# A hand-written order for the opening of a decoder layer, and a raised priority for one chain in its down stage

## The chip, the core and the metric

The kernel runs on one core of a Trainium2 chip. The time is that of the device for one execution, in microseconds (us). An execution under the profiler gives the trace; its own time is listed beside the runs without it.

## What is computed

One decoder layer on 512 tokens of width 1024, in float32: a half-step SwiGLU feed-forward, a mixer (block-sparse attention beside a state-space model), and a second half-step feed-forward, each between two RMS norms.

```python
def swiglu(x, w_gate, w_up, w_down):
    return (jax.nn.silu(x @ w_gate) * (x @ w_up)) @ w_down

f = swiglu(rmsnorm(h, ffn1_pre_g[l]), ffn1_w_gate[l], ffn1_w_up[l], ffn1_w_down[l])
h = h + 0.5 * rmsnorm(f, ffn1_post_g[l])
```

The hidden width is 2816, that is 22 blocks of 128. The state-space model needs tables that depend on its parameters alone: among them the powers 1 to 128 of a complex number for each of 2048 states. They are computed in the first feed-forward, between its own instructions.

## The kernel before

Every product is split in two parts for precision. A float32 operand becomes a high part (ScalarE, a copy to a narrower format) and a low part (VectorE, the operand minus its high part), and a product is three matmuls: high by high, high by low, low by high. A weight of 128 by 1024 comes by DMA into one of three raw buffers (`load`, L76) and is split by `weight` (L82): L89 on ScalarE, L90 on VectorE. A raw buffer is free for the next load when its low part has been made.

**The opening** (L1139 to L1182) handles the first two hidden blocks, that is four weights (gate and up of block 0, gate and up of block 1), called units here. The tokens lie in four blocks of 128. `turn_x` (L135) transposes the rows of one token block, in two halves of 512 columns: four transposes on TensorE, a product by the column gain on VectorE (L143), the high part on ScalarE (L145); `low_x` makes the low part. The first two token blocks are not normalised before the products: their rows are turned as they come, and their norm factor is applied later. The last two are normalised first: `norm_x` (L153) squares the rows and adds them up (`square`, on ScalarE, or on VectorE for block 3), makes the factor with a power on GpSimd (L60), scales the rows on ScalarE (L163), and gives a function that turns them.

`halves` (L214) multiplies the units in two halves of 256 tokens: first tokens 0 to 255 for all four units, then tokens 256 to 511. Its hooks turn token block 2 after the first half of unit 1, and block 3 after that of unit 2. The first half of unit 0 goes by parts, all eight high by high products, then high by low, then low by high; the others take the three products of each of the eight slices in turn. Between the halves stands `late_norm` (L179): a diagonal of the norm factors is spread over all partitions by a product with ones (L188), copied out by ScalarE (L190), then the four PSUM banks are multiplied by it (L192), then the columns of the first two token blocks (L196), whose parts are made anew (L197, L198) for the hidden blocks that follow. A unit's two halves lie in the two halves of one bank.

**The order** of TensorE and GpSimd is that of the program. VectorE, ScalarE and the DMA queue of SP are ordered by a planner, which simulates the program with costs of its own and gives each engine the ready instruction that stands first; `high_priority(PRIO)` counts an instruction as standing 400 places earlier. Within `manual_schedule` (L1156) the instructions of VectorE and ScalarE keep the program's order among themselves.

**The down stage** (L484 to L500) takes the 22 hidden blocks one by one: `split` makes the parts of a hidden block (L475 on ScalarE, L476 on VectorE), `weight` those of its down weight, and TensorE issues 24 matmuls of 512 columns into eight banks. After each block the loop draws steps from a generator, here `rest` (L710): three after the first block, two after the second, then one each. It first makes the powers by doubling, in eight steps of six VectorE instructions each (`cmul`, L557; the result is named e, its scratch ett), stores them to DRAM (L731), then makes four tables (st) from loads (f, b). From the twelfth block on, the parts of hidden blocks lie in memory that the powers held (`open_third`, L267).

Of the kernel before, what the change touches and what calls it, by code (L numbers as in the profile page):

```python
# [25 lines left out]
class Core:  # L26
    def __init__(self, tc, ctx):
# [7 lines left out]
        self.ident = self.const.tile([P, P], F32, name="ident")  # L35
# [93 lines left out]
    def open_x(self, ctx, gcol):  # L129
# [3 lines left out]
        self.gcol = gcol  # L133

    def turn_x(self, t, q, rows):  # L135
# [9 lines left out]
        nc.scalar.activation(self.xh[:, k, t * P:(t + 1) * P], f, AF.Copy)  # L145
# [6 lines left out]

    def norm_x(self, t, on_dve=False):  # L153

        nc = self.nc
        ss = self.small("ss", 2)
        xn = [self.t512("xn") for _ in range(2)]
        with self.tc.high_priority(PRIO):
            for q in range(2):
                self.square(t, q, xn[q], ss, on_dve)  # L160
            rs = self.rsqrt(ss, D * EPS)
            for q in range(2):
                nc.scalar.activation(xn[q], self.h[t][:, 512 * q:512 * q + 512], AF.Copy, scale=rs)  # L163

        def transposes():
            with self.tc.high_priority(PRIO):
                for q in range(2):
                    self.turn_x(t, q, xn[q])
                    self.low_x(t, q)
        return transposes  # L170
# [8 lines left out]
    def late_norm(self, banks):  # L179
# [4 lines left out]
        diag = self.t512("diag")  # L184
        for t in range(2):
            v.tensor_scalar(diag[:, t * P:(t + 1) * P], self.ident, self.rs[t], None, op0=OP.mult)
# [4 lines left out]
        for b in banks:  # L191
            v.tensor_tensor(b[:, :H], b[:, :H], rsb, OP.mult)  # L192
        for q in range(2):
# [4 lines left out]
            v.tensor_tensor(self.xl[:, k, :H], f, self.xh[:, k, :H].bitcast(F32), OP.subtract)  # L198

# [14 lines left out]
    def halves(self, units, hooks, by_part=False):  # L214


        for half in range(2):
            for i, (u, pb) in enumerate(units):
                if half == 0 and i == 0 and by_part:
                    pairs = ((u[0], self.xh), (u[0], self.xl), (u[1], self.xh))  # L220
                    for n, (a, b) in enumerate(pairs):
                        for k in range(NK):
                            self.nc.tensor.matmul(pb[:, :H], a[:, k * P:(k + 1) * P], b[:, k, :H],
                                                  start=n == 0 and k == 0, stop=n == 2 and k == NK - 1)
                else:
                    self.proj_T(u, pb, (half * H, half * H + H))
# [3 lines left out]
            if half == 0 and by_part:  # L230
                self.late_norm([pb for u, pb in units])
# [200 lines left out]
    def ffn(self, wgu, wd, gains, tail, hooks, first, direct, store=None):  # L432
# [19 lines left out]
        us = [(u, self.bank("gu")) for u in first]  # L452
# [34 lines left out]
        for i, k in enumerate(order):  # L487
# [11 lines left out]
            for _ in range({0: 3, 1: 2}.get(i, 1)):  # L499
                next(self.filler or iter(()), None)  # L500
# [66 lines left out]
class Tables:  # L567
# [142 lines left out]
    def rest(self, pool, wide, vec):  # L710
# [9 lines left out]
        while n < P:  # L720
            for lo in range(0, n, 32):
                m = min(32, n - lo)
                s1, s2 = (t[:, :16 * m].rearrange("p (c x) -> p c x", c=16) for t in tt)
                cmul(vec, et[0][:, :, n + lo:n + lo + m], et[1][:, :, n + lo:n + lo + m],
                     et[0][:, :, lo:lo + m], et[1][:, :, lo:lo + m],
                     et[0][:, :, n - 1:n].to_broadcast([P, 16, m]), et[1][:, :, n - 1:n].to_broadcast([P, 16, m]), s1, s2)
# [373 lines left out]
def _lay(i):  # L1100
    a = {k: np.asarray(v)[0] for k, v in i.items()}
    win, wo = a["w_in"], a["w_out"]
    out = dict(x=a["x"], ident=np.eye(P, dtype=np.float32))
# [5 lines left out]
    out["g0col"] = a["ffn1_pre_g"].reshape(NK, P).T  # L1109
# [23 lines left out]
def layer(tc, ctx, a, out):  # L1133
# [6 lines left out]
    nc.sync.dma_start(c.ident, a["ident"])  # L1140
    gcol = c.const.tile([P, NK], F32, name="gcol")
# [14 lines left out]
    with tc.manual_schedule(engines={mybir.EngineType.DVE, mybir.EngineType.Activation}):  # L1156
# [10 lines left out]
        for q in range(2):  # L1167
            for t in range(2):
                c.low_x(t, q)
# [47 lines left out]
```

## Time and profile before

| | |
|---|---|
| median of 3 runs | 936.06 us (934.13 to 937.15) |
| the profiled execution | 932.66 us, span 930.7 us |
| TensorE busy | 910.2 us, 98% of the span |
| VectorE busy | 688.8 us, 74% |
| ScalarE busy | 426.5 us, 46% |
| GpSimd busy | 58.8 us, 6% |
| mean granted TensorE clock | 0.992 |

The span runs from the first instruction of the program to the last. Engines are named as in the profile: PE is TensorE's matmuls (transposes too), PEld its weight loads, DVE VectorE, ACT ScalarE, POOL GpSimd, SP the queue that issues the DMAs. L12 is line 12 of the kernel; the line can be that of a helper. In a row of a timeline, x4 says that four like instructions were merged, and the brackets give the idle time of the engine ahead of the first of them and who ended it. The durations of neighbours overlap by a little, so the distance of their starts is shorter than a duration. A granted clock of 1.00 is 2.4 GHz, one of 0.50 is 1.2 GHz.

### The profile page before, as it was taken

Reading aid. Unit: us, or ns where it says so; the run is one execution under the profiler, and the core shown is the slowest. Engines: PE = TensorE matmul, PEld = TensorE weight load, DVE = VectorE, ACT = ScalarE, POOL = GpSimd, SP = SyncE. Lnnn points to the kernel's source line nnn. Section 1 sums busy time; section 2 is a strip of 40 time slices with the busy share of each in tenths; the row PEclk is TensorE's granted clock in tenths of the full one; section 3 lists DMA queues with packets and bytes.
Section 4 is the critical chain, followed back from the end, with each engine's and each line's share of the span. In section 5 each row is a group of like instructions: output and inputs, shape, how many; then the busy total and the mean of one; then the engine's idle time right before and its main releaser. Section 6 shows DMA issues by size and latency. Waiting matters only on the chain.

```text
span 930.7 us, 14874 instructions
## 1 busy us (share of the span) xinstructions
PE 910.2 (98%) x5815; PEld 816.6 (88%) x5815; DVE 688.8 (74%) x1179; ACT 426.5 (46%) x717; POOL 58.8 (6%) x47
## 2 busy tenths in 40 slices
PE   7899999999999899998999999999999999999997
PEld 6888899999988788987888778989999999988885
DVE  6998678888588655579999869698878887533623
ACT  5622345455422444333478756445445555423511
POOL 0600000000000001022120113000000000000000
PEclk9999999999999999999999999999999999999999
DMA  7444532332666651584433132322433333332402
GB/s 262 122 135 130 186 101 91 108 98 69 192 178 216 224 187 35 171 249 147 147 98 97 32 105 71 121 82 91 117 111 100 106 102 104 116 110 90 136 1 90
DMA packets 51718, 114.59 MB, mean 123 GB/s; under 512 B 10048, under 2 KB 21056, under 8 KB 51648
## 3 DMA queue, kind: packets, MB, share of 16 engines
q1 hardware_dynamic: 51648, 113.65, 38.9%
q8 instruction: 45, 0.74, 0.3%
q14 instruction: 25, 0.20, 0.1%
HBM read 102.62 MB, written 11.01 MB: 122 GB/s over the span
## 4 chain that ended last, share of the span: by engine, by line
PE 79%; DVE 11%; DMA 3%; ACT 3%; issue 2%; POOL 1%; SPq 1%; DVEq 0%; POOLq 0%; ACTq 0%
PE c L408 28%; PE d L204 6%; PE d L202 6%; PE d L203 6%; PE p L408 5%; DMA b<-in_bturn 2%; PE pg L202 2%; PE pu L204 2%; PE pg L204 2%; PE pu L203 2%; PE pg L203 2%; PE pu L202 2%; DVE w L90 1%; PE gu L204 1%; PE gu L202 1%
## 5 line engine op out<-in xcount | busy, mean ns | idle before, releaser
L408 PE MATMUL c<-xh,w 128*128 128x256 f32 x1024 | 180.7, 277 | 0.2 <-DVE w L287 0.2
L408 PEld LDWEIGHTS c<-xh,w 128*128 128x128 f32 x1024 | 157.0, 188 | 0.5 <-DVE w L287 0.4
L90 DVE TENSOR_TENSOR w<-w,w 128x1024 fp32r<-128x1024 f32 x93 | 114.8, 1241 | 44.6 <-ACT w L89 44.3
L89 ACT ACTIVATE w<-w 128x1024 fp32r<-128x1024 f32 x93 | 97.3, 1054 | 101.6 <-PE d L204 20.0
L408 PE MATMUL c<-xl,w 128*128 128x256 f32 x512 | 141.7, 277 | 0.0
L204 PE MATMUL d<-w,sl 128*128 128x512 f32 x352 | 137.6, 391 | 2.5 <-DVE sl L476 2.5
L202 PE MATMUL d<-w,sh 128*128 128x512 f32 x352 | 137.8, 392 | 0.0
L203 PE MATMUL d<-w,sh 128*128 128x512 f32 x352 | 137.7, 391 | 0.0
L287 DVE TENSOR_TENSOR w<-w,w 128x1024 fp32r<-128x1024 f32 x96 | 116.7, 1221 | 27.5 <-ACT w L286 27.1
L286 ACT ACTIVATE w<-w 128x1024 fp32r<-128x1024 f32 x96 | 100.2, 1058 | 67.6 <-PE c L408 40.8
L408 PE MATMUL c<-t,w 128*128 128x256 f32 x768 | 97.4, 283 | 0.1
L408 PEld LDWEIGHTS c<-xl,w 128*128 128x128 f32 x512 | 96.2, 188 | 0.0
L408 PEld LDWEIGHTS c<-t,w 128*128 128x128 f32 x768 | 94.1, 191 | 0.3 <-DVE w L287 0.3
L204 PEld LDWEIGHTS d<-w,sl 128*128 128x128 f32 x352 | 66.5, 189 | 16.8 <-DVE sl L476 2.9
L202 PEld LDWEIGHTS d<-w,sh 128*128 128x128 f32 x352 | 66.4, 189 | 13.8
L203 PEld LDWEIGHTS d<-w,sh 128*128 128x128 f32 x352 | 66.5, 189 | 13.6
L60 POOL TENSOR_TENSOR rs<-v,mhalf 128x1 f32<-128x1 f32 x24 | 19.1, 799 | 715.2 <-DVE v L56 715.2
L408 PE MATMUL p<-t,s1h 128*128 128x256 f32 x256 | 46.5, 282 | 0.0
L475 ACT ACTIVATE sh<-late 128x512 fp32r<-128x512 f32 x22 | 13.5, 630 | 60.9 <-PE d L203 60.9
L468 ACT ACTIVATE sg<-c 128x256 f32<-128x256 f32 x64 | 24.5, 382 | 34.1 <-DVE c L426 27.6
L408 PEld LDWEIGHTS p<-t,s1h 128*128 128x128 f32 x256 | 39.6, 190 | 0.0
L408 PE MATMUL p<-t,s1l 128*128 128x256 f32 x128 | 36.1, 282 | 0.0
(318 smaller groups left out, 1778.7 us busy)
## 6 DMA issues: line engine op xcount, KB each, us to landing
w<-in_wgu SPq DMA_DIRECT2D x88, 512.0 KB, 3.5
w<-in_wd SPq DMA_DIRECT2D x44, 512.0 KB, 3.7
e<-e SPq DMA_DIRECT2D x16, 256.0 KB, 3.5
w<-in_wq SPq DMA_DIRECT2D x8, 512.0 KB, 3.7
g<-in_gains SPq DMA_DIRECT2D x5, 512.0 KB, 6.0
h<-in_x SPq DMA_DIRECT2D x4, 512.0 KB, 6.0
ca<-cx SPq DMA_DIRECT2D x8, 256.0 KB, 4.4
f<-win SPq DMA_DIRECT2D x32, 64.0 KB, 3.7
```

What stands on the lines that cost most here:

```text
L60: self.nc.gpsimd.tensor_tensor(rs, v, self.mhalf, OP.pow)
L89: nc.scalar.activation(hi, raw, AF.Copy)
L90: (eng or nc.vector).tensor_tensor(lo, raw, hi.bitcast(F32), OP.subtract)
L202: nc.tensor.matmul(out, ah, bh, start=first, stop=False)
L203: nc.tensor.matmul(out, ah, bl, start=False, stop=False)
L204: nc.tensor.matmul(out, al, bh, start=False, stop=last)
L286: nc.scalar.activation(hi, src, AF.Copy)
L287: nc.vector.tensor_tensor(lo, src, hi.bitcast(F32), OP.subtract)
L408: nc.tensor.matmul(out, l[:, s], r[:, kb + k, t], start=first and k == 0 and n == 0, stop=last and k == 3 and n == 2, skip_group_check=True)
L468: nc.scalar.activation(sg, pg, AF.Silu)
L475: nc.scalar.activation(hi, hidden[k], AF.Copy)
```

## The change

The opening is written out in one order for VectorE and ScalarE; the squares of token block 0 stand before its first high parts, those of block 1 near the end, the squares of blocks 2 and 3 between the parts of weights 1 and 2. `turn_x` no longer makes the high part; `high_x` does, as a step of its own. The first halves of all four units are issued there, each by parts (`first_half`), and token blocks 2 and 3 are turned inside those of units 2 and 3, after their high by high products. `halves` then does only the second halves, and `late_norm` comes after that of unit 0, with raised priority; in it the four banks are multiplied after the columns and no longer before. The column gains come with the identity in one DMA. In the down stage the steps of the powers get raised priority, and four steps are drawn after the first block.

```diff
+    def high_x(self, t, q):
+        k = slice(4 * q, 4 * q + 4)
+        f = self.xf[t // 2][:, k, t % 2 * P:t % 2 * P + P]
+        self.nc.scalar.activation(self.xh[:, k, t * P:(t + 1) * P], f, AF.Copy)
...
         rsb = self.t512("rsb")[:, :H]
         nc.scalar.activation(rsb, pb, AF.Copy)
-        for b in banks:
-            v.tensor_tensor(b[:, :H], b[:, :H], rsb, OP.mult)
         for q in range(2):
             k = slice(4 * q, 4 * q + 4)
             f = self.xf[0][:, k]
             v.tensor_tensor(f, f, rsb.unsqueeze(1).to_broadcast([P, 4, H]), OP.mult)
             nc.scalar.activation(self.xh[:, k, :H], f, AF.Copy)
             v.tensor_tensor(self.xl[:, k, :H], f, self.xh[:, k, :H].bitcast(F32), OP.subtract)
+        for b in banks:
+            v.tensor_tensor(b[:, :H], b[:, :H], rsb, OP.mult)
...
+    def first_half(self, unit, pb, between=None):
+
+        hi, lo = unit
+        for n, (a, b) in enumerate(((hi, self.xh), (hi, self.xl), (lo, self.xh))):
+            for k in range(NK):
+                self.nc.tensor.matmul(pb[:, :H], a[:, k * P:(k + 1) * P], b[:, k, :H],
+                                      start=n == 0 and k == 0, stop=n == 2 and k == NK - 1)
+            if n == 0 and between is not None:
+                between()
+
+    def halves(self, units, hooks, begun=False):
...
+        for half in range(begun, 2):
             for i, (u, pb) in enumerate(units):
...
+                self.proj_T(u, pb, (half * H, half * H + H))
...
+                if begun and i == 0:
+                    with self.tc.high_priority(PRIO):
+                        self.late_norm([pb for u, pb in units])
...
-            for _ in range({0: 3, 1: 2}.get(i, 1)):
+            for _ in range({0: 4, 1: 2}.get(i, 1)):
                 next(self.filler or iter(()), None)
...
+                with core.tc.high_priority(PRIO):
+                    cmul(vec, et[0][:, :, n + lo:n + lo + m], et[1][:, :, n + lo:n + lo + m],
...
-    nc.sync.dma_start(c.ident, a["ident"])
-    gcol = c.const.tile([P, NK], F32, name="gcol")
-    nc.sync.dma_start(gcol, a["g0col"])
+    nc.sync.dma_start(c.identg, a["ident"])
...
+        c.turn_x(0, 0, rows(0, 0))
+        c.turn_x(0, 1, rows(0, 1))
         for q in range(2):
+            c.square(0, q, junk, ss[0], False)
+        c.high_x(0, 0)
+        c.high_x(0, 1)
+        warm_up(WARM[1])
+        c.turn_x(1, 0, rows(1, 0))
+        c.turn_x(1, 1, rows(1, 1))
+        warm_up(WARM[2])
+        c.high_x(1, 0)
+        high(0, col(0))
+        c.high_x(1, 1)
+        high(0, col(1))
         for q in range(2):
             for t in range(2):
                 c.low_x(t, q)
+        banks = [c.bank("gu") for j in range(4)]
+        low(0, col(0))
+        low(0, col(1))
+        c.first_half(w[0], banks[0])
+        high(1)
         for q in range(2):
+            c.square(2, q, xn[2][q], ss[2], False)
+        for q in range(2):
+            c.square(3, q, xn[3][q], ss[3], True)
+        rs2 = c.rsqrt(ss[2], D * EPS)
+        low(1)
+        rs3 = c.rsqrt(ss[3], D * EPS)
+        c.first_half(w[1], banks[1])
+        high(2)
+        scaled(2, rs2)
+        low(2)
+        c.first_half(w[2], banks[2], turn(2))
+        high(3)
+        low(3)
+        for q in range(2):
+            c.high_x(2, q)
+        for q in range(2):
+            c.low_x(2, q)
+        scaled(3, rs3)
+        for q in range(2):
+            c.square(1, q, junk, ss[1], False)
+        c.first_half(w[3], banks[3], turn(3))
+        for q in range(2):
+            c.high_x(3, q)
+        rs = [c.rsqrt(ss[t], D * EPS) for t in range(2)]
+        for q in range(2):
+            c.low_x(3, q)
+        c.diag = c.t512("diag")
         for t in range(2):
+            v.tensor_scalar(c.diag[:, t * P:(t + 1) * P], c.ident, rs[t], None, op0=OP.mult)
+        first = list(zip(w, banks))
```

Here `high(j)` and `low(j)` make the parts of unit j's weight, `scaled(t, rs)` scales the rows of token block t, and `turn(t)` turns them.

## Rows read from the trace of the kernel before

**Rows 1.** The page, part 1: busy us (share of the span) xinstructions

```profile
PE 910.2 (98%) x5815; PEld 816.6 (88%) x5815; DVE 688.8 (74%) x1179; ACT 426.5 (46%) x717; POOL 58.8 (6%) x47
```

**Rows 2.** Waits of TensorE, whole span: us in total, times, longest us

```profile
PE d L204 <- DVE sl L476: 2.5, 1, 2.5
PE gu L204 <- DVE w L90: 1.7, 3, 1.1
PE tp L140 <- ACT xn L163: 1.6, 1, 1.6
PE gu L223 <- ACT first L1166: 1.5, 1, 1.5
PE gu L202 <- DVE gu L192: 0.9, 1, 0.9
```

**Rows 3.** Busy us by stretch, opening: length, engines (xinstructions), clock, DMA share, GB/s

```profile
10.00:13.00 3.00, 2.93 (x24) 2.92 (x25) 3.00 (x6) 2.71 (x7) 0.00 (x0) 1.00 0.84 335
13.00:42.30 29.30, 24.77 (x189) 23.13 (x189) 23.34 (x44) 18.79 (x29) 11.49 (x7) 0.94 0.49 139
...
25.00:26.00 1.00, 0.50 (x3) 0.50 (x4) 1.00 (x2) 1.00 (x3) 0.00 (x0) 0.82 0.51 80
...
28.00:29.00 1.00, 1.00 (x7) 1.00 (x7) 0.64 (x3) 0.00 (x0) 1.00 (x2) 0.50 0.41 164
```

**Rows 4.** Timeline, TensorE: start us, us, instruction [idle before <-releaser]

```profile
31.28 0.38 PE L202 MATMUL gu<-xh,first 128*128 128x256 f32 x1 [0.94 <-DVE gu L192]
...
42.28 0.39 PE L202 MATMUL pg<-xh,w 128*128 128x512 f32 x1
```

**Rows 5.** Timeline of the down stage, VectorE and SP

```profile
251.04 1.22 DVE L90 TENSOR_TENSOR w<-w,w 128x1024 fp32r<-128x1024 f32 x1
...
305.07 0.68 DVE L564 TENSOR_TENSOR e<-ett 128x512 f32<-128x512 f32 x1
...
305.78 2.18 SPq L731 DMA_DIRECT2D e<-e  x4
...
311.23 2.54 DVE L476 TENSOR_TENSOR sl<-h,sh 128x512 fp32r<-128x512 f32 x4 [2.60 <-DMA e<-e]
```

**Rows 6.** Busy us by stretch, instructions on the down stage's banks alone

```profile
309.40:316.00 6.60, 4.15 (x12) 3.17 (x12) 0.00 (x0) 0.00 (x0) 0.74 0.66 229
```

**Rows 7.** Timeline of the opening, VectorE

```profile
11.16 1.28 DVE L1171 TENSOR_TENSOR first<-w,first 128x512 fp32r<-128x512 f32 x2
...
30.79 1.43 DVE L192 TENSOR_TENSOR gu<-gu,rsb 128x256 f32<-128x256 f32 x4 [1.28 <-ACT rsb L190]
32.12 2.35 DVE L196 TENSOR_TENSOR xf<-xf,rsb 128x1024 f32<-128x1024 f32 x2
...
34.49 1.22 DVE L311 TENSOR_TENSOR xf<-xf,xf 128x1024 f32<-128x1024 f32 x1
35.63 1.22 DVE L198 TENSOR_TENSOR xl<-xf,xh 128x1024 fp32r<-128x1024 f32 x1
```

**Rows 8.** Timeline of the opening, ScalarE

```profile
6.33 1.23 ACT L145 ACTIVATE xh<-xf 128x512 fp32r<-128x512 f32 x2 [4.32 <-DVE xf L143]
...
10.44 1.05 ACT L89 ACTIVATE w<-w 128x1024 fp32r<-128x1024 f32 x1
11.39 0.62 ACT L177 ACTIVATE xn<-h 128x512 f32<-128x512 f32 x1
...
14.34 1.34 ACT L163 ACTIVATE xn<-h,rs 128x512 f32<-128x512 f32 x2 [1.63 <-POOL rs L60]
```

**Rows 9.** Timeline of the opening, SP

```profile
12.47 5.78 SPq L79 DMA_DIRECT2D w<-in_wgu  x3
```

**Rows 10.** Timeline of the opening, GpSimd

```profile
13.72 0.58 POOL L60 TENSOR_TENSOR rs<-v,mhalf 128x1 f32<-128x1 f32 x1 [13.28 <-DVE v L56]
20.46 1.05 POOL L60 TENSOR_TENSOR rs<-v,mhalf 128x1 f32<-128x1 f32 x1 [6.15 <-DVE v L56]
```

**Rows 11.** Sum of six stretches from 247 to 307 us, instructions on e

```profile
sum 60.00, DVE 18.75 POOL 0.00; mean DVE 3.12 POOL 0.00
```

More of the change, by code (lines that the diff above doesn't have):

```diff
@@ L151, in low_x @@
         self.nc.vector.tensor_tensor(self.xl[:, k, c], f, self.xh[:, k, c].bitcast(F32), OP.subtract)
[L153 to L170, printed above, removed]
     def square(self, t, q, junk, ss, on_dve):
@@ L183, in late_norm @@
         v = nc.vector
-        diag = self.t512("diag")
-        for t in range(2):
-            v.tensor_scalar(diag[:, t * P:(t + 1) * P], self.ident, self.rs[t], None, op0=OP.mult)
+        diag = self.diag
         pb = banks[-1][:, H:]
@@ L451, in ffn @@
         NS = 2
-        us = [(u, self.bank("gu")) for u in first]
+        us = [u if self.xf is not None else (u, self.bank("gu")) for u in first]
         self.halves(us, hooks, self.xf is not None)
@@ L1149, in layer @@
     warm = c.bank("warm")
-    c.open_x(sx, gcol)
+    c.open_x(sx)
     def warm_up(n):
@@ L1157, in layer, with high, low, scaled @@
         warm_up(WARM[0])
-        nc.vector.tensor_scalar(gcol, gcol, 32.0, None, op0=OP.mult)
-        for t in range(2):
-            for q in range(2):
-                c.turn_x(t, q, c.h[t][:, 512 * q:512 * q + 512])
-            warm_up(WARM[1 + t])
-        w0 = [c.wp.tile([P, 1024], F32R, tag=f"w{i}", name=f"first{i}") for i in (1, 2)]
-        col = lambda q: slice(512 * q, 512 * q + 512)
-        for q in range(2):
-            nc.scalar.activation(w0[0][:, col(q)], raws[0][:, col(q)], AF.Copy)
+        v, act = nc.vector, nc.scalar
+        v.tensor_scalar(c.gcol, c.gcol, 32.0, None, op0=OP.mult)
+        rows = lambda t, q: c.h[t][:, 512 * q:512 * q + 512]
+        col = lambda q: slice(512 * q, 512 * q + 512)
+        ss = [c.small("ss", 2) for t in range(4)]
+        junk = c.t512("junk")
+        xn = {t: [c.t512("xn") for q in range(2)] for t in (2, 3)}
+        w = [[c.wp.tile([P, 1024], F32R, tag=f"w{i}", name=f"first{j}{i}") for i in (1, 2)] for j in range(4)]
+        def high(j, c=slice(0, 1024)):
+            act.activation(w[j][0][:, c], raws[j][:, c], AF.Copy)
+        def low(j, c=slice(0, 1024)):
+            v.tensor_tensor(w[j][1][:, c], raws[j][:, c], w[j][0][:, c].bitcast(F32), OP.subtract)
+        def scaled(t, rs):
+            for q in range(2):
+                act.activation(xn[t][q], rows(t, q), AF.Copy, scale=rs)
+        def turn(t):
+            return lambda: [c.turn_x(t, q, xn[t][q]) for q in range(2)]
+        c.turn_x(0, 0, rows(0, 0))
+        c.turn_x(0, 1, rows(0, 1))
+        for q in range(2):
+            c.square(0, q, junk, ss[0], False)
[9 more added lines that the diff above has]
+        high(0, col(1))
         for q in range(2):
```

41 lines of the change are left out of this document (8 added, 33 removed).

## The prediction

> **What bounds the kernel now.** I read part 1 of the page first: TensorE is busy 910.2 of 930.7 us [rows 1], so time can only come out of its 20.5 us of idle, or out of stretches in which its clock is low. The list of its waits comes next [rows 2]. The reader should see that they are few and that most of them lie in two places: in the opening (1.7 us for low parts of weights, 1.6 us for the scaled rows of the second half, 0.9 us for the scaled banks) and once in a down stage (2.5 us for a split). The granted clock by stretch is third, because a wait has a second price: from 25.6 to about 29 us TensorE runs at 0.50, the 1.2 GHz level, after the waits between 20.7 and 25.5 us [rows 3].
>
> How much the opening loses is a subtraction. Between 13.00 and 42.30 us [rows 3] TensorE issues seven half products of 24 matmuls, 16 transposes and the sums that spread the late norm. At full clock a 256-column matmul follows the last one after about 0.1145 us (18 of them lie between 14.09 and 16.14 us on its timeline), so 168 cost 19.2 us; the transposes take 1.7, the spreading sums 0.5: 21.4 us of work in 29.3. The loss is 7.9 us. About 1.5 of it is half clock (20 matmuls took 3.8 us instead of 2.3), the rest are waits with the refilling behind each. All of the next stage begins where this stretch ends, at 42.28 us [rows 4], and TensorE then works without a break until the down stage, so a microsecond won before 42.28 is a microsecond won at the end.
>
> In the down stage the chain is: the last operation of the powers ends at 305.75 us, the store of e that follows them lands at 311.1, and the split that takes over their memory starts only then [rows 5]. From 309.40 to 316.00 us TensorE gets through 12 matmuls of 512 columns [rows 6], which at its 0.227 us pace would be 2.7 us: 3.9 us are lost, 2.45 as the wait and the rest at 0.50 of the clock.
>
> **The change, part by part.** *The first unit (to 13 us).* The column gains ride with the identity, one DMA issue of 0.4 us less on SP; the squares of block 0 take ScalarE while it waits for its first input (idle 4.3 us before 6.33 [rows 8]), so they cost nothing; without that cover they would push the first high parts back by their 1.5 us. The last link is unchanged: the low parts of the first weight end on VectorE at 12.44 us [rows 7], four matmuls later the unit is over, 12.95 us. The earlier issue is worth 0 to 0.4 us; I take 0.
>
> *Units 1 to 3.* I carried the hand-written orders forward with the durations of [rows 7, 8]: on ScalarE a 1024-column copy takes 1.05 us, a square 0.62 and two of them with their read-outs about 1.5, a scaling of two halves 1.34; on VectorE 1024 columns take 1.14 to 1.22, 512 columns 0.64. Unit 1: high part on ScalarE to 11.6, squares of block 2 to 13.1; VectorE squares block 3 to 13.7 and makes the low part to 14.95, against 14.8 when TensorE has done the two parts that need none: 0.2 us of wait. Unit 1 ends at 15.95. ScalarE: second weight to 14.15, scaled rows of block 2 from 14.45 to 15.8. Unit 2: first part to 16.9, the transposes of block 2 find their rows ready, end 19.65, its low part done at 16.2. The fourth raw weight is issued at 12.47 us as now [rows 9] and lands some 3.6 us later, so its high part ends about 17.3 and its low part 19.9. Block 3 is scaled by 20.7, when unit 3 has just done its first part (20.6); it ends at 23.35. The columns of block 3 are multiplied to 22.4, their high parts follow to 23.4, their low parts to 24.05. The second half of unit 0 can start at 23.4 and ends at 26.2, the spreading sums at 26.8; the diagonal is due at 24.9. What goes is thus the wait for the scaled rows and for the last low parts, and with them the half clock of this place: without a new wait the three remaining half products (8.2 us) would end at 35.0 instead of 42.3.
>
> *The new wait.* The norm factor now comes after the second half of unit 0, and in it the banks are scaled after the columns, not before. Today TensorE's first matmul of a second half waits 0.94 us for VectorE's scaling of the same bank, though they touch different halves of it [rows 4]. So units 1, 2 and 3 will each wait for their bank. VectorE's order there is the planner's: the raised priority puts these steps ahead of others, by program order among themselves. From the end of the spreading sums to a scaled bank is 0.94 us; a column product costs 1.17 (2.35 for two), a low part 1.14, a bank 0.36 [rows 7]. Banks first: 0.94 + 0.36 = 1.3 us (low end). Both products, then banks: 0.94 + 2.35 + 0.36 = 3.65. Both products and both low parts first: 5.9, and 7.0 if ScalarE does the high part of a new weight (1.05) ahead of the spread factor (high end). I take 3.65: in the trace another instruction of 1.2 us stands between the second product and the first low part [rows 7], so the planner holds the low part, which waits for ScalarE, to be not yet ready there, and a bank is what is ready. The waits of 2.45 us and of 20.7 to 25.5 us each brought the half clock [rows 3, 6], those of 0.94 and 1.5 us did not [rows 2 to 4], so I add 1.5 us. TensorE: 26.8 + 3.65 + 8.25 + 1.5 = 40.2 us against 42.3, a gain of 2.1. Bounds: 36.3 (gain 5.9) and 43.5 (loss 1.2).
>
> On the hand-written chain stand four calls of GpSimd for the norm factors, among VectorE work that is denser than now. One took 0.58 us while VectorE had a gap, 1.05 while it made low parts [rows 10]; with 1.05 for each the scaled rows of block 2 come at 16.3, still ahead of 16.9, and the diagonal at 25.4, ahead of 26.2. The Trainium skill ("SBUF — State Buffer", section on the shared port pair) has a harder rule: GpSimd and a VectorE operation with two SBUF inputs exclude each other for a whole instruction. By that rule each call could lie behind one more operation of 1.2 us, which the two rows, apart by 0.5 us, bear out in part.
>
> *The down stage.* The powers (48 products, 18.75 us of VectorE busy time [rows 11]) go ahead of splits, weight parts and the state tables in the planner's order, and one more step of them is released at the first block. Now they share VectorE with the tables, step by step in turn. I expect them to end 10 to 20 us earlier, since dependent products leave gaps into which splits and weight parts fall, as they do in the trace. 3.3 us earlier is enough to bring the store home before the split is needed; beyond that nothing is won. Next late are the tables themselves, which end at 306.35 now and gate nothing that TensorE needs before the mixer. Gain: 0 to 3.9 us; I take 3.9, since the wait has this one cause.
>
> **Sum.** 2.1 + 3.9 = 6.0 us off the profiled execution, 932.66 us (span 930.7), gives 926.7. The runs shown have a median of 936.06, 3.4 above that execution; the prediction is for such a median: 936.06 - 6.0 = 930.1.
>
> **Rivals.**
> 1. *Banks first.* If the planner finds the banks ready before the products, or VectorE sees them in time, the new wait is 1.3 us and brings no half clock: 5.9 + 3.9 = 9.8, 926.3 us. For it: today they do come first. Against: program order now puts them last.
> 2. *Banks last.* Low parts too go first, and perhaps a new weight's high part: the wait is 5.9 to 7.0 us, the opening gains -0.1 to -1.2, and all that is left is the down stage: about 932.8 us.
> 3. *GpSimd holds the chain.* If each factor of blocks 0 and 1 has to let one more VectorE operation of 1.2 us pass, the diagonal comes at 27.4 instead of before 26.2 and the late norm moves by 1.2 us: 931.3 us. Against: the two calls of [rows 10] differ by 0.5 us, not by 1.2. The rule of the Trainium skill named above would have it so.
> 4. *The powers don't free the store.* SP issues in order, and the store of e stands behind whatever the planner put ahead of it; if it still lands after 309 us only the opening's 2.1 count: 934.0 us.
> 5. *Slower: the powers shut out the weights.* If they run as one block from 249.3 us, of some 16 us (18 products of 512 columns 0.60 us apart, the 30 shorter ones 5), the low parts of the third and fourth blocks' weights, the last of them begun at 251.0 now [rows 5], come after 265.3. TensorE reaches the third block at 249.0 + 2 x 5.44 = 259.9, waits 5.4 us and 1.2 for the part itself, and pays 1.5 of half clock: 8.1 lost, 3.9 won. With a late norm at its high end (1.2 lost) that is 5.4 slower, with the forecast one 2.1 slower: 938.2 to 941.5 us, say 940. It decides once the block keeps VectorE for more than 10.6 us without letting a weight part in. Against it: between dependent products the planner lets others through now.
>
> **How the numbers follow.** Forecast 0.36, rival 1 0.17, rival 2 0.18, rival 3 0.05, rival 4 0.11, rival 5 0.13. The likeliest gives 930.1 us. Its own range, with the new wait between 3.2 and 5 us, is 927.5 to 932.5. The wide range must reach rival 1 on one side and rivals 2 and 4 on the other, with a little for the planner's order later in the program, which moves with any change of its picture: 925 to 937.5, which leaves rival 5 and the tails out. A measurement of this kernel tells about 0.3% (2.8 us) from no change. Faster by more: the forecast, rivals 1 and 3 and a third of rival 2, less some scatter, 0.62. Within: the rest of rival 2 and rival 4, 0.25. Slower: rival 5, 0.13.
>
> **What would show it.** Right: no wait of TensorE over 0.5 us between 13 and 26 us and a clock of 1.00 there; one new wait of 3 to 5 us for a bank's scaling near 27 us with half clock behind it; the first 512-column product of the next block near 40 us; the powers ended before 295 us and no wait of a down-stage matmul for its split. Wrong: a wait behind the fourth weight or the diagonal, a low part of a weight that TensorE waits for near 260 us, or waits in the mixer that the kernel before does not have.

## The result: slower by 0.8%

The changed kernel took 943.03 us (median; 942.61 to 943.75), the kernel before 936.12 (934.13 to 937.15): ratio 1.0082, interval 1.0064 to 1.0101. The profiled execution took 942.61 us, its span is 940.6. The forecast was 930.1. The two profiled executions lie further apart (9.9 us of span) than the medians (6.9). One profiled execution below, run 1's, had a granted clock of 0.752 from start to end and took 1120.44 us, so no row of it is used.

Part 1 of the page after, against [rows 1]:

```profile
PE 918.6 (98%) x5815; PEld 824.7 (88%) x5815; DVE 689.0 (73%) x1179; ACT 427.8 (45%) x717; POOL 54.8 (6%) x47
```

The same 5815 matmuls keep TensorE busy 8.4 us longer. So most of the loss is not waiting: the work itself runs slower. Among the largest groups of matmuls are the pairs: the later hidden blocks of both FFNs (feed-forwards), two at a time, multiplied 256 columns at a time into banks named c. What streams past the weights there is xh or xl (the high and low parts of the tokens) or t (sums of them, in tiles of their own). The groups, shapes kept apart (busy us, mean ns of one | idle before), first of the kernel before:

```profile
L408 PE MATMUL c<-xh,w 128*128 128x256 f32 x1024 | 180.7, 277 | 0.2 <-DVE w L287 0.2
L408 PE MATMUL c<-xl,w 128*128 128x256 f32 x512 | 141.7, 277 | 0.0
L408 PE MATMUL c<-t,w 128*128 128x256 f32 x768 | 97.4, 283 | 0.1
```

and of the changed one:

```profile
L396 PE MATMUL c<-xh,w 128*128 128x256 f32 x1024 | 187.2, 281 | 0.1
L396 PE MATMUL c<-xl,w 128*128 128x256 f32 x512 | 143.8, 281 | 0.0
L396 PE MATMUL c<-t,w 128*128 128x256 f32 x768 | 97.4, 283 | 0.1
```

The matmuls are slower where xh or xl streams past the weights, and not slower where t does. The chain that ended last merges a run of 144 of them, 96 on xh or xl and 48 on t, into one row (start us, us); before, then after:

```profile
117.99 16.66 PE c L408 x144
```

```profile
118.24 17.11 PE c L396 x144
```

The 0.45 us between them, put on the 96, are 4.7 ns each. By the distance of starts on TensorE's timeline a matmul on xh or xl takes 113.9 ns before and 118.4 after, one on t 119.6 and 119.7. By the same starts the first FFN's pairs take 140.3 us instead of 137.3, the second's 180.8 instead of 177.3: 6.5 us in all. No line of code that the change touches runs in either place.

The waits of TensorE, against [rows 2]:

```profile
PE gu L185 <- DVE gu L181: 5.4, 1, 5.4
...
PE d L185 <- ACT sh L463: 2.4, 1, 2.4
PE d L187 <- DVE sl L464: 1.9, 1, 1.9
PE gu L202 <- ACT first L1155: 1.2, 2, 0.9
...
PE gu L171 <- DVE diag L1218: 0.2, 1, 0.2
```

The opening's old waits between 13 and 26 us are gone (that for the first weight stays, 1.2 us for 1.5); one new wait of 5.4 us stands in their place, and the down stage has two waits for a split where it had one. (A wait in the mixer, which [rows 2] leaves out, is 2.7 us before and 2.4 after.) The opening on the timelines of TensorE, ScalarE and VectorE, against [rows 4, 7]:

```profile
26.25 0.70 PE L171 MATMUL gu<-diag,const-float32-1.0 128*128 128x256 f32 x2 [0.15 <-DVE diag L1218]
32.30 0.58 PE L185 MATMUL gu<-xh,first 128*128 128x256 f32 x1 [5.35 <-DVE gu L181]
```

```profile
26.02 1.06 ACT L90 ACTIVATE w<-w 128x1024 fp32r<-128x1024 f32 x1 [3.09 <-PE gu L186]
26.99 0.38 ACT L173 ACTIVATE rsb<-gu 128x256 f32<-128x256 f32 x1
```

```profile
28.00 1.22 DVE L91 TENSOR_TENSOR w<-w,w 128x1024 fp32r<-128x1024 f32 x1
29.22 2.35 DVE L177 TENSOR_TENSOR xf<-xf,rsb 128x1024 f32<-128x1024 f32 x2
31.49 1.42 DVE L181 TENSOR_TENSOR gu<-gu,rsb 128x256 f32<-128x256 f32 x4
```

Read downwards they give the wait. ScalarE copies the spread factor out as soon as the sums end (26.95 us), so a new weight's high part ahead of it costs nothing. On VectorE small steps of the state-space model and that weight's low part go ahead of the column products, which begin 1.85 us after the factor is there (27.37 to 29.22), and the banks come last. The clock by stretch (as in [rows 3]) shows no trouble before and the price behind:

```profile
13.00:26.25 13.25, 12.99 (x109) 12.59 (x108) 10.12 (x23) 8.49 (x15) 6.66 (x5) 1.00 0.84 235
...
30.00:36.00 6.00, 3.70 (x17) 3.70 (x18) 6.00 (x11) 4.94 (x5) 4.38 (x2) 0.51 0.80 262
36.00:42.00 6.00, 6.00 (x53) 6.00 (x52) 6.00 (x11) 3.45 (x4) 0.00 (x0) 1.00 0.01 3
```

The first product of the next block starts at 42.51 us (before 42.28). In the down stage the stores of e leave SP in one row of eight; before, they left in two rows of four, the second of which is in [rows 5]. The first of these on SP's timeline of before, then SP's row after:

```profile
300.43 1.87 SPq L731 DMA_DIRECT2D e<-e  x4
```

```profile
307.35 5.46 SPq L721 DMA_DIRECT2D e<-e  x8
```

and the two waits that it makes, on ScalarE and TensorE:

```profile
313.93 0.63 ACT L463 ACTIVATE sh<-h 128x512 fp32r<-128x512 f32 x1 [6.06 <-DMA e<-e]
316.46 1.67 ACT L463 ACTIVATE sh<-h 128x512 fp32r<-128x512 f32 x3 [1.90 <-DMA e<-e]
```

```profile
314.61 0.50 PE L185 MATMUL d<-w,sh 128*128 128x512 f32 x1 [2.40 <-ACT sh L463]
317.23 0.79 PE L187 MATMUL d<-w,sl 128*128 128x512 f32 x1 [1.88 <-DVE sl L464]
```

The end of the powers on VectorE shows why the rows have joined. The real part's stores can leave when L561 (after: L549) has run, the imaginary part's when L564 (L552) has. Before, the first of the two:

```profile
299.72 0.69 DVE L561 TENSOR_TENSOR e<-ett 128x512 f32<-128x512 f32 x1
```

and both of them after:

```profile
306.63 0.69 DVE L549 TENSOR_TENSOR e<-ett 128x512 f32<-128x512 f32 x1
308.68 0.69 DVE L552 TENSOR_TENSOR e<-ett 128x512 f32<-128x512 f32 x1
```

Before, other work stood between the two, which ended 5.35 us apart; after, it stands ahead of both, and they end 2.05 us apart.

The stage began 3.2 us later than before (252.2, the pairs' loss) and its length to the mixer's first product is 128.8 us instead of 125.9.

### The profile page after: what moved, and what is told of

Its sections match the earlier page's. It is cut to its first block, busy times and chain, and to the rows that moved or that the text cites. A ratio compares the mean times of both kernels' runs of the same rounds, so it can differ in the third digit from the quotient of the medians.

```text
span 940.6 us, 14870 instructions
## 1 busy us (share of the span) xinstructions
PE 918.6 (98%) x5815; PEld 824.7 (88%) x5815; DVE 689.0 (73%) x1179; ACT 427.8 (45%) x717; POOL 54.8 (6%) x47
## 4 chain that ended last, share of the span: by engine, by line
PE 81%; DVE 8%; DMA 5%; ACT 2%; SPq 2%; issue 2%; POOL 0%; DVEq 0%; POOLq 0%; ACTq 0%
PE c L396 28%; PE d L187 6%; PE d L186 6%; PE d L185 6%; PE p L396 5%; DMA b<-in_bturn 2%; PE pg L185 2%; PE pg L187 2%; PE pu L187 2%; PE pu L185 2%; PE pg L186 2%; PE pu L186 2%; PE wo L187 1%; PE wo L185 1%; PE wo L186 1%
## 5 line engine op out<-in xcount | busy, mean ns | idle before, releaser
L396 PE MATMUL c<-xh,w 128*128 128x256 f32 x1024 | 187.2, 281 | 0.1
L396 PEld LDWEIGHTS c<-xh,w 128*128 128x128 f32 x1024 | 159.3, 189 | 0.3 <-DVE w L275 0.3
L90 ACT ACTIVATE w<-w 128x1024 fp32r<-128x1024 f32 x90 | 94.3, 1055 | 108.9 <-PE d L187 22.5
L396 PE MATMUL c<-xl,w 128*128 128x256 f32 x512 | 143.8, 281 | 0.0
L91 DVE TENSOR_TENSOR w<-w,w 128x1024 fp32r<-128x1024 f32 x90 | 111.3, 1243 | 41.2 <-ACT w L90 41.0
L275 DVE TENSOR_TENSOR w<-w,w 128x1024 fp32r<-128x1024 f32 x96 | 116.9, 1222 | 29.4 <-ACT w L274 28.8
L274 ACT ACTIVATE w<-w 128x1024 fp32r<-128x1024 f32 x96 | 100.2, 1058 | 72.5 <-PE c L396 45.3
```

Source lines behind the costliest of these rows:

```text
L90: nc.scalar.activation(hi, raw, AF.Copy)
L91: (eng or nc.vector).tensor_tensor(lo, raw, hi.bitcast(F32), OP.subtract)
L274: nc.scalar.activation(hi, src, AF.Copy)
L275: nc.vector.tensor_tensor(lo, src, hi.bitcast(F32), OP.subtract)
L396: nc.tensor.matmul(out, l[:, s], r[:, kb + k, t], start=first and k == 0 and n == 0, stop=last and k == 3 and n == 2, skip_group_check=True)
```

## Experiments: what slows the matmuls on xh and xl

The change also holds these lines:

```diff
-        self.ident = self.const.tile([P, P], F32, name="ident")
+        self.identg = self.const.tile([P, P + NK], F32, name="ident")
```

The merged tile for identity and gains is 544 bytes per partition long, the identity alone was 512. It is allocated ahead of h, xh and xl, and the gains used to stand behind them: so these three lie 32 bytes further on, and the weights don't. That was theory A.

**Run 1**, the kernel before with only the tile lengthened; all behind it moves, the weights too:

```diff
-        self.ident = self.const.tile([P, P], F32, name="ident")
+        self.identw = self.const.tile([P, P + 8], F32, name="ident")
+        self.ident = self.identw[:, :P]
```

> The kernel before, with 8 unused columns behind the 128 of the identity: h, xh and xl lie 32 bytes further on in SBUF, nothing else differs. In the profile of the changed kernel the pairs' matmuls that read xh and xl ran 4 to 5 ns apart longer (144 of them 17.11 us against 16.66), those that read other tiles did not. Theory A, the place of xh and xl sets that pace: 144 pair matmuls in about 17.1 us, time 940 to 944 us. Rival B, the pace comes from the new order of the opening or from which banks and weight slots its work takes: 16.7 us, 936 us within 1.5.

Measured: 935.46 us, ratio 1.0006 (0.9985 to 1.0026). Nothing lost, so theory A as put falls.

**Run 2**, the changed kernel, the tile allocated behind xl:

```diff
-        self.identg = self.const.tile([P, P + NK], F32, name="ident")
...
         self.xl = self.const.tile([P, NK, S], F32R, name="xl")
+        self.identg = self.const.tile([P, P + NK], F32, name="ident")
...
```

> The changed kernel with the merged identity and gain tile placed behind xh and xl instead of ahead of h: h, xh and xl lie 544 bytes lower than in the changed kernel, on a multiple of 64 as before the change. Theory A (place of xh and xl sets the pace): 144 pair matmuls back at about 16.7 us, 7 us come back in the profile, time 935 to 939 us; what is left over 936 is the down stage's new wait. Rival B (the order of the opening sets the pace): 17.1 us, 943 us within 1.5.

Measured: 936.05 us, ratio 1.0019 (1.0004 to 1.0034), a row of 144 in 16.66 us. Rival B falls: the changed order runs at the old pace. What is left is the distance between xh and xl on the one hand and the weights, or something else that lies behind xl, on the other.

**Run 3**, the kernel before with 32 unused bytes between xl and the weights; **run 4**, the changed kernel with the same 32 bytes:

```diff
         self.mhalf = self.const.tile([P, 1], F32, name="mhalf")
+        self.pad = self.const.tile([P, 8], F32, name="pad")
```

> The kernel before, with 32 unused bytes between xh, xl and the weight pool: xh and xl stay on a multiple of 64 bytes, the weights and all that lies behind them start 32 bytes past one. The first run moved both by 32 and its time stayed at 935.5 us, so the place of xh and xl alone (theory A as first put) is out. Theory A2: what counts is that the two operands of a matmul start at different remainders of 64 bytes. It expects 144 pair matmuls c<-xh, c<-xl at about 17.1 us instead of 16.66, the products of other tiles with weights (c<-t, d) unchanged since both lie in the moved part, and 940 to 944 us. Rival B (the pace comes from the new opening): 16.66 us and 935 us within 1.5.

> The changed kernel with the same 32 unused bytes behind xl: xh, xl and the weights all start 32 bytes past a multiple of 64, so the two operands agree again, while the merged tile and the changed order stay as they are. A2: 144 pair matmuls at 16.66 us, 936 us within 1.5 (as the changed kernel with its merged tile moved behind xl, 936.05). Rival A3, that xh and xl must lie on a multiple of 64 once the weights are read in the changed order: 17.1 us, 943 us.

Run 3: 943.2 us, ratio 1.0097 (1.0078 to 1.0117), rows of 17.12 us. Run 4: 935.18 us, ratio 1.0016 (1.0004 to 1.0028). One and the same edit makes the old kernel slow and the changed one fast. Run 4's chain:

```profile
118.19 16.66 PE c L397 x144
```

**Runs 5 to 7**, the kernel before with small tiles allocated ahead of xh (32, 64 and 1408 bytes), the weights unmoved (the lines of three edits; the comments are not in the kernels):

```diff
+        self.mhalf = self.const.tile([P, 1], F32, name="mhalf")        # run 5
+        self.gc = self.const.tile([P, NK], F32, name="gcol")           # run 6, with the line above
+        self.sm = self.const.tile([P, 16, 22], F32, name="ssm_small")  # run 7, alone
         self.xh = self.const.tile([P, NK, S], F32R, name="xh")
```

> The kernel before with one 4-byte constant, which takes 32 bytes, allocated ahead of xh instead of behind xl: xh and xl 32 bytes further on, h, the weights and everything else where they were. Theory A2 (operands at different remainders of 64 bytes slow the matmuls): 144 pair matmuls at 17.1 us and 940 to 944 us, as with the weights moved instead. Rival A4 (what slowed the earlier run was something else behind the weight pool that moved with it): 16.66 us, 934 to 936 us.

> The same with the 32 bytes of the column gains ahead of xh too: xh and xl 64 bytes further on, all else where it was. If the remainder of 64 bytes is what counts: 16.66 us per 144 pair matmuls, 934 to 936 us. If the remainder of a larger size counts (128 bytes, where this run differs from the kernel before and from the run with the merged tile behind xl): 17 us or more, 940 us.

> The kernel before with the 1408-byte tile of the small state constants allocated ahead of xh instead of behind xl: xh and xl 1408 bytes further on, h, the weights and all behind them unmoved. From xh to the weights it is then 64 bytes modulo 128 as before, but 192 modulo 256 (before: 64). Theory A5 (64 modulo 128 is the fast distance): 144 pair matmuls at 16.66 us, 933 to 936 us. Rival A6 (any move of xh off its place modulo 256 or 512 slows it): 17.1 us or more, 941 to 944 us.

Run 5: 942.52 us, ratio 1.0082 (1.0054 to 1.0110); in the kernel before the 32 bytes alone cost 0.8%. Run 6: 943.3 us, 1.0103 (1.0057 to 1.0149), so A2's remainder of 64 bytes is wrong. Run 7: 939.12 us, 1.0043 (1.0021 to 1.0065), so A5's 64 modulo 128 is wrong too; its pace is what A6 expects, its time lies below A6's 941 to 944. The chain of run 6:

```profile
118.47 17.28 PE c L409 x144
```

All runs by the bytes in a partition from xh's start to the first slot of the weights' high parts, added up from the tiles that the programs allocate between them (the same from xl to the low parts):

| kernel | bytes | modulo 512 | row of 144, us |
|---|---|---|---|
| before; run 4 | 67904 | 320 | 16.66 |
| run 1 | 67904 | 320 | no row used, time as before |
| run 2 | 68416 | 320 | 16.66 |
| changed; run 5 | 67872 | 288 | 17.11 |
| run 3 | 67936 | 352 | 17.12 |
| run 6 | 67840 | 256 | 17.28 |
| run 7 | 66496 | 448 | 17.07 |

Shown: a distance sets the pace, since moving xh and xl costs it, moving the weights with all that lies behind xl costs it, and moving both gives it back. That it is the distance to the weights is argued: they are the other operand of these matmuls, and the matmuls on t, which moved with the weights in every run, keep 119.6 to 120.0 ns. Traffic of others is not it: in the changed kernel the matmuls on xh and xl follow at 118.2 to 118.6 ns with VectorE and ScalarE busy or idle beside them, and at 118.3 with a DMA under way or none. Which rule of the distance does it is open; the one remainder of 512 that is known to be fast occurred at two distances, four others are slower by 0.41 to 0.62 us a row. Nor does the same distance suit every product: the 512-column products of xh with weights (pg) follow at 233.9 ns before, 234.0 in the changed kernel, but 227.6 in run 6 and 230.2 in run 7, whose pairs are slow.

## Experiments: the opening and the down stage apart

**Run 8**, the kernel before with the down stage's two edits alone; **run 9**, run 2 without them, that is, the new opening alone. The edits, as run 8 has them:

```diff
-            for _ in range({0: 3, 1: 2}.get(i, 1)):
+            for _ in range({0: 4, 1: 2}.get(i, 1)):
...
+                with core.tc.high_priority(PRIO):
                     cmul(vec, et[0][:, :, n + lo:n + lo + m], ...
```

> The kernel before with the two edits of the down stage alone (priority for the powers, four steps ahead of the first store instead of three). The prediction's step: powers end 10 us earlier, the stores of e land before the split: 932 us. Rival from the profile of the changed kernel: the powers take the same 57 us from the stage's start, all eight stores of e issue in one row and the split of h waits up to 6 us for them: 2 to 3 us lost, 938 to 939 us. Second rival: the stores' order matters to no one, 936 within 1. Pairs at 16.7 us per 144 matmuls under A and B alike.

> The changed kernel with the merged tile behind xh and xl and the two edits of the down stage undone: the new opening alone. In the profile of the changed kernel the next block began at 42.51 us against 42.28 before, so the opening by itself gains nothing: under A 936 us within 1.5, pairs at 16.7 us per 144; under B 940 to 941, pairs at 17.1. Against the run with the down stage's edits in: 2 to 3 us less if these cost what the trace shows, 4 more if the prediction was right about them.

Run 8: 935.95 us, 1.0009 (0.9992 to 1.0026). Run 9: 932.5 us, 0.9973 (0.9958 to 0.9989). The forecast's 3.9 us for the down stage are not there. On the old opening the two edits change the time by nothing that can be told; on the new one they cost 936.05 - 932.5 = 3.6 us.

**Runs 10 and 11**, run 9 with the priority alone and with the fourth step alone.

> The new opening as the change has it (merged tile behind xl) with the priority alone. It stands between the run without either edit (932.5 us) and with both (936.05). Theory E: no loss from the priority alone, 929 to 933 us. Rival G (the priority is the loss): 935 to 937 us.

> The same with the fourth step alone. Theory E: no loss, 929 to 933 us. Rival H (the step is the loss): 935 to 937 us. If both this and the priority alone are at 932 to 933 and both together at 936, the two edits cost only together.

Run 10: 933.32 us, 0.9978 (0.9963 to 0.9993), no loss. Run 11: 935.52 us, 1.0004 (0.9989 to 1.0020), the loss: rival H. TensorE's down stage in run 11:

```profile
314.97 0.72 PE L185 MATMUL d<-w,sh 128*128 128x512 f32 x1 [3.18 <-ACT sh L463]
317.70 0.79 PE L187 MATMUL d<-w,sl 128*128 128x512 f32 x1 [1.58 <-DVE sl L464]
```

and the stretch from 306 to 321 us, run 9 and then run 11 (columns as in [rows 3]):

```profile
306.00:321.00 15.00, 12.51 (x56) 10.04 (x55) 11.32 (x15) 7.41 (x11) 0.00 (x0) 1.00 0.65 227
```

```profile
306.00:321.00 15.00, 10.24 (x36) 7.53 (x35) 10.30 (x14) 5.76 (x9) 0.00 (x0) 0.80 0.74 263
```

Two waits instead of one (and one of 0.87 us ahead of them), and the clock falls to half behind them (0.50 from 316 to 320 us): 36 matmuls against 56 in the same 15 us.

**Runs 12 and 13** take run 9's opening further: the banks scaled ahead of the columns, and behind all second halves. The lines that move are those of the banks in late_norm; in run 13 they come back at the end of halves:

```diff
-        for b in banks:
-            v.tensor_tensor(b[:, :H], b[:, :H], rsb, OP.mult)
...
+        if begun:
+            with self.tc.high_priority(PRIO):
+                for u, pb in units:
+                    self.nc.vector.tensor_tensor(pb[:, :H], pb[:, :H], rsb, OP.mult)
```

> The new opening alone (merged tile behind xl, down stage as before), with the late norm's four bank products ahead of its columns. In the opening alone TensorE waited 5.56 us for the last bank product, then ran to 37.8 us at the half clock. Theory (this wait and the half clock behind it are what ate the opening's gain): the wait shrinks by the two column products of 2.36 us, and by the half clock's share if the clock holds; the next block starts at 38.5 to 40.5 us instead of 42.9, time 929 to 931 us. Rival: the next block waits for its weights and for the columns, which are later now, and starts at 42 us or later: 932 us.

> The new opening alone with the four bank products behind all the second halves in program order. Theory: TensorE has no wait between the spreading sum and the second halves of units 1 to 3 and ends them near 34.5 us at full clock; the next block starts at 35.5 to 38 us instead of 42.9, time 925 to 929 us. Rival: the bank products then sit behind other VectorE work, the sigmoids start later, and TensorE waits for the next block's banks or weights until 41 us or later: 931 to 933 us.

Run 12: 929.45 us, 0.9951 (0.9933 to 0.9968); its wait is 3.08 us and the next block starts at 40.7, just behind the 38.5 to 40.5 expected. Run 13: 926.87 us, 0.9919 (0.9900 to 0.9939); no wait, next block at 34.97. From 30 to 36 us TensorE issues 20 matmuls in run 9, and in run 12 and run 13:

```profile
30.00:36.00 6.00, 5.21 (x31) 5.22 (x32) 6.00 (x11) 3.64 (x4) 5.32 (x2) 0.72 0.77 251
```

```profile
30.00:36.00 6.00, 5.51 (x46) 5.19 (x45) 6.00 (x11) 5.90 (x7) 4.34 (x2) 1.00 0.70 223
```

Both theories hold: the wait for the banks, and the half clock behind it, ate the opening's gain. Run 13's interval lies below run 9's; run 12's overlaps it.

**Runs 14 to 16** are run 13 with the priority alone, the fourth step alone, and both.

> The fastest so far (new opening, bank products last, merged tile behind xl, down stage as before: 926.9 us, ratio 0.9919) with the powers' priority alone. In its profile VectorE stands still five times, 8.5 us in all, before a product of the states' tables whose load has not landed (2.29, 3.09 us), with the powers queued behind it. Theory D (the powers are held by those loads, and priority only pushes the state products and with them their loads back): powers end no earlier, all eight stores of e in one row, 2 to 3 us slower, 929 to 930 us. The prediction's step: powers 5 us or more earlier, 923 us. Rival: the loss sits in the fourth step, not in the priority: 927 us.

> The same fastest kernel with four steps ahead of the second row instead of three and no priority. Theory D: the steps only say how early the powers may be placed, and VectorE has room there: powers and stores within 1 us of the kernel without it, 926 to 928 us. The prediction's step: part of the 3.9 us, 925 us or less. Rival (the loss of the down stage's edits sits here): 929 to 930 us.

> The kernel with the bank products last, with both edits of the down stage (priority and the fourth step). Theory E (each alone lets four of the eight stores of e or all of them issue earlier, but the two together push all state products ahead of the last power, so that the eight stores issue in one row after it, as in the changed kernel): 3 us slower than either alone, 926 to 929 us, and the row of eight stores begins 57 to 58 us after the stage's first product. Rival F (the loss hangs on the opening, which shifts the stage against the loads): both together as good as each alone, 921 to 924 us, stores begin 53 to 55 us after it.

Run 14: 923.7 us, 0.9890 (0.9869 to 0.9912), with run 15 the fastest kernel here. Run 15: 923.85 us, 0.9892 (0.9868 to 0.9917). Their intervals overlap run 13's, so a gain of 0.3% on it is likely and not shown. Theory D's loss on the first did not come, and both times are those of the prediction's step; but the powers end only 1.1 us earlier in run 14, not 5, so that agreement is luck. The stall that D names is there, as this row of run 13 on VectorE shows, but priority doesn't lengthen it (2.06 us in run 14):

```profile
261.79 0.69 DVE L550 TENSOR_TENSOR st<-f,b 128x512 f32<-128x512 f32 x1 [3.09 <-DMA b<-in_bturn]
```

Run 16: 926.05 us, 0.9893 (0.9872 to 0.9914), by its ratio as good as either alone, which speaks for F, as the begin of its stores does; its median lies in E's range. Its one profiled execution is longer there than run 13's (table below) and, at 927.48 us, near the slow end of its runs, 923.41 to 927.67: on the faster opening the step's effect stays unsettled.

**Runs 17 and 18** make the powers really early. In run 17 the state products use the powers' scratch tile, so that none can come between them; run 18 spends the freed space on a second buffer for the state tables' loads.

```diff
-            t = [pool.tile([P, 512], F32, tag=f"st{j}", name=f"st{j}_{q}") for j in range(2)]
-            cmul(vec, *st, *f, *b, *t)
+            cmul(vec, *st, *f, *b, *tt)
```

> The fastest kernel with the state products written through the powers' own scratch tile, so that none of them can be placed between the powers: VectorE has no load to wait for until the last power is done. It makes the powers really early, which the change's priority was forecast to do. Theory D: powers end 15 us or more earlier (by 283 us instead of 298), the stores of e have landed before the split, but the four groups of state tables, each with 4 us of issue, a load and 3.6 us of products in single buffers, now follow one after another and end at 305 us or later: the split waits for them instead, and the time is 926 to 930 us. The prediction's step (powers early is what counts): the wait of 5.4 us on the split goes, 923 to 924 us.

> As the run with the state products behind the powers, with the freed scratch space used for a second buffer of the state tables' larger loads, so that a group's loads issue before the products of the one before are done. If the state tables' loads set the end there, this brings 2 to 4 us against it, 923 to 925 us; if the stores of e or the order on VectorE does, nothing.

Run 17: 940.63 us, 1.0078 (1.0052 to 1.0104); run 18: 930.29 us, 0.9967 (0.9952 to 0.9983). In run 17 the stores of e issue from 274.4 to 279.7 us, some 19 us earlier than in run 13, and TensorE then waits for the split longer than ever, because the tables are what is last (in its profiled execution, which took 948.43 us):

```profile
PE d L186 <- DVE sl L467: 16.0, 1, 16.0
```

D had the mechanism (powers early, tables last) but 10 us too little of the loss; the prediction's 923 to 924 is far off. A second buffer takes 10.3 us back, more than the 2 to 4 expected, and still leaves it 3.4 us behind run 13 (0.5% by the ratios). Powers that end early are worth nothing once they push the tables back.

The down stage in these kernels, in us from its first product, one execution each (last row of stores: when SP begins it; lowest clock: the granted clock, lowest of the stretches of 2 us from 58 to 80 us; length: to the mixer's first product):

| kernel | step, priority | stores | last row | lowest clock | length |
|---|---|---|---|---|---|
| before | 3, no | 4 + 4 | 56.7 | 0.50 | 125.9 |
| run 9 | 3, no | 4 + 4 | 56.9 | 1.00 | 124.3 |
| run 12 | 3, no | 4 + 4 | 55.4 | 1.00 | 122.4 |
| run 10 | 3, yes | 4 + 4 | 55.3 | 1.00 | 123.0 |
| run 13 | 3, no | 4 + 4 | 56.7 | 0.50 | 125.9 |
| run 14 | 3, yes | 4 + 4 | 55.5 | 1.00 | 123.2 |
| run 15 | 4, no | 8 | 53.1 | 0.50 | 125.7 |
| run 16 | 4, yes | 8 | 54.6 | 0.50 | 128.3 |
| changed | 4, yes | 8 | 55.2 | 0.50 | 128.8 |
| run 8 | 4, yes | 8 | 55.7 | 0.50 | 128.9 |
| run 2 | 4, yes | 8 | 56.5 | 0.50 | 129.4 |
| run 11 | 4, no | 8 | 57.5 | 0.50 | 130.4 |

Every kernel with the fourth step has the row of eight, none without it. In these traces a row of eight costs 3.5 to 6.5 us against a second row of four that begins within 0.3 us of it. The times bear that out on run 9's opening (run 11, 2.9 us by the ratios), but not on run 13's (run 15 is no slower) nor on the old one (run 8). The clock is part of these lengths. TensorE's wait for the split is 2.49 us in run 9 and in run 13; the 6 us that begin 1 us before its end, run 9 and then run 13 (columns as in [rows 3]):

```profile
311.60:317.60 6.00, 4.97 (x22) 4.13 (x23) 5.57 (x8) 4.19 (x7) 0.00 (x0) 1.00 0.57 192
```

```profile
304.30:310.30 6.00, 5.01 (x15) 3.96 (x16) 5.57 (x8) 4.18 (x7) 0.00 (x0) 0.72 0.54 179
```

One paid half clock for the same wait, the other did not: that is the 1.6 us between their lengths, and it is part of the 2.7 us between runs 13 and 14. What the priority alone is worth is open: on run 9's opening the times show nothing (run 10), and run 12, without it, has its stores as early.

## Why the prediction was wrong

**The step that failed most** is "the column gains ride with the identity, one DMA issue of 0.4 us less on SP", taken at 0. It counted the DMA and not the tile: 32 bytes between xh and the weights cost 1.0082 against 1.0019 in run 2, 0.6% or 5.9 us, and 0.8% in the kernel before (run 5). No view of the profile of before hints at it, but the diff says that a tile grows ahead of operands of nearly every product.

**Units 1 to 3: right.** Forecast 23.35 us for the end of unit 3, no wait over 0.5 us and a clock of 1.00; the trace has the spreading sums at 26.25 (forecast 26.2) behind a wait of 0.15 us, and 1.00. Rival 3 is out: GpSimd held nothing up. Its four calls took 0.64 to 1.45 us (1.05 each in the working), and the wait for the diagonal is 0.15 us, not 1.2. Whatever the Trainium skill's rule of the exclusive port pair ("SBUF — State Buffer", "Who interferes with whom") did to these calls, it cost TensorE no more than that here.

**The new wait: right in place and cause, too small.** 3.65 us was forecast, 5.35 came. The term that was too small is the time from the factor to VectorE's first use of it: 0.03 us before, 1.85 now, for small steps and the new weight's low part on VectorE (1.22), which weren't in the sum. ScalarE's high part ahead of the factor, which the upper bound named at 1.05, cost nothing: the factor began 0.04 us after the sums. The half clock behind the wait is 17 matmuls in 3.7 us from 32.30 on, which take 2.0 at full clock, so 1.7 (forecast 1.5). The next block thus started at 42.51, not 40.2. In time the opening alone (run 9) gained 0.27%, 2.5 us (1.0 to 3.9), near the forecast's 2.1; but its profiled execution doesn't show them in the opening, where its next block starts at 42.9. So the agreement is luck, and where the gain comes from is open.

**The down stage: wrong in sign.** "I expect them to end 10 to 20 us earlier": the last power ended 57.2 us after the stage's start (309.37 - 252.2), before 56.7 (305.75 - 249.04). State products that wait for their loads stand between the powers on VectorE. And the premise that an early end is what frees the split was half the matter: the stores of the real and the imaginary parts used to leave 5.35 us apart, and the fourth step put them into one row, for the first half 3.7 us later (307.35 - 252.2 against 300.43 - 249.0). The term's half clock was no fixed price either: behind a wait of 2.49 us it came in run 13 and not in run 9. Rival 4 named the store, but not that it could get worse. Rival 5 didn't come: TensorE waits for no weight near 260 us.

**The sum.** Forecast -2.1 - 3.9 = -6.0. Measured by ratios: opening -2.5 (run 9), down stage +4.3 (run 2 against run 9, 0.46%), placement +5.9: +7.7, that is 0.82%, against the +6.9 of the medians. The three close by construction, and the split depends on the order: on the old opening the down stage's edits cost nothing in time (run 8) and the 32 bytes 0.8% (run 5). No rival held the outcome, since the largest term was in none; rival 5, the only slower one, named another cause.

## What to carry to other kernels

When a diff changes a tile's size, list what is allocated behind it, and after the run compare the pace of untouched matmuls before looking for waits. An instruction in a high-priority group isn't ahead of what is ready earlier: between a wait's two ends reckon with what the engine has at hand, here 1.85 us of it. Where a split waits for stores, look at when each half of them leaves, not only the last one. Don't read a difference of 2 us between two single executions as an edit's worth before the granted clock behind their waits has been compared.

## What the runs showed of the hardware

A 256-column matmul of the pairs on xh or xl starts 113.9 ns after the last one, or 118 to 120 (runs 3, 5, 6 and 7), as the distance of xh and xl from the weights and what lies with them in a partition has it, with the same instructions. The Trainium skill ("SBUF — State Buffer", "Who interferes with whom") gives TensorE two independent read ports, one for the moving operand and one for weight loads, and lets only the pair shared by VectorE and GpSimd cause contention. That rule has no price for the distance; runs 3 and 5 to 7 measured 0.4 to 1.0% of the kernel, and the measurement decides. Whether reads collide after all, or what else ties pace to distance, was not tried.
